# Add and GELU on one core: larger DMA rows, all loads ahead of all stores, and the adds on GpSimd

## The chip, the core and the metric

The kernel runs on one core of a Trainium2 chip. A core has several engines that run side by side, each with its own instruction stream: VectorE (DVE in the profile), ScalarE (ACT), GpSimd (POOL), TensorE (PE, not used here), and SyncE (SP), which here issues all DMA transfers. The transfers run on 16 DMA engines. Data lives in SBUF (128 partitions) and in PSUM, a smaller memory that VectorE and ScalarE can use too.

The metric is the device time of one execution, in microseconds (us). The kernel before has a median of 126.06 us over 11 runs (124.79 to 126.96).

## The reference

x and y are float32 arrays of 1024 rows by 4096 columns. The output has the same shape.

```python
z = x + y
out = 0.5 * z * (1 + tanh(sqrt(2 / pi) * (z + 0.044715 * z ** 3)))
```

This is the tanh form of GELU. Since 0.5 (1 + tanh(u)) = sigmoid(2u), it is z * sigmoid(c1 * z + root**2 * z**3), with c1 = 2 sqrt(2 / pi) and root**2 = c1 * 0.044715. The kernel computes it in this form.

## The kernel before, in words

Each partition holds 8 rows of an input one after the other, so 8 x 4096 = 32768 columns of float32 per partition, in one contiguous stretch of HBM (128 KB). The kernel cuts these columns into transfers and, within them, into chunks.

**Transfers.** The list `sizes` has 13 stretches of columns: 1024, 1024, 2048, six of 4096, 2048, 1024, 512, 512. Each stretch is loaded once from x (`load_x`, L73) and once from y (`load_y`, L80), and stored once (`store`, L83). A stretch of 4096 columns is 2 MB in rows of 16 KB, one row per partition. Each x stretch has its own resident tile, which the computation overwrites and which is then stored. y goes into four buffers of 4096 columns used in turn (`YB = 4`).

**Chunks.** The computation works on chunks of up to 1024 columns, 33 of them. For chunk c:

- `add` (L92): z = x + y, written over x. On GpSimd, except for the first two and the last two chunks, which are on VectorE (`by_pool`).
- `sq` (L97): ScalarE writes (root * z)**2 into a PSUM buffer w, of which there are four.
- `stt` (L100): VectorE makes w = (w + c1) * z.
- `sig` (L105): ScalarE makes w = sigmoid(w).
- `mul` (L108): VectorE writes z = w * z, over x.

**Order.** The order within each queue is written out by hand. ScalarE and VectorE follow a skewed order:

```python
for i in range(-3, C + 1):
    if 0 <= i < C:
        dve.append((stt, i))
        acts.append((sig, i))
    if 0 <= i - 1 < C:
        dve.append((mul, i - 1))
    if 0 <= i + 3 < C and i + 3 not in by_pool:
        dve.append((add, i + 3))
    if 0 <= i + 2 < C:
        acts.append((sq, i + 2))
```

So in ScalarE's queue the square of chunk i+1 stands ahead of the sigmoid of chunk i, and in VectorE's queue stt of i+1 stands ahead of mul of i. GpSimd has its adds in order of chunks.

SyncE's single queue holds loads and stores mixed: x and y of a stretch, then each store whose stretch ends at least `LEAD` = 8192 columns before the end of what has been loaded. A store that waits for its last mul holds up the loads behind it on this queue. The dictionary `needs` lists what each step must have behind it when the order is emitted; the semaphores between the engines are placed automatically, by the overlap of the regions that instructions read and write.

Of the kernel before, what the change touches and what calls it, by code (L numbers as in the profile page):

```python
# [1 line left out]

# [1 line left out]

# [4 lines left out]


@with_exitstack
def kernel(
    ctx: ExitStack,
    tc: tile.TileContext,
    x: bass.AP,
    y: bass.AP,
    out: bass.AP,
):

    nc = tc.nc
    P = nc.NUM_PARTITIONS
    fp32 = mybir.dt.float32
    act = mybir.ActivationFunctionType
    alu = mybir.AluOpType  # L30

    N, D = x.shape
    assert N % P == 0
    NB = N // P
    TOT = NB * D

    c1 = 2.0 * math.sqrt(2.0 / math.pi)
    root = math.sqrt(c1 * 0.044715)

    LEAD = 8192  # L40
    CH = 1024
    YB = 4
    sizes = [1024, 1024, 2048] + [D] * (NB - 2) + [2048, 1024, 512, 512]
    assert sum(sizes) == TOT
    starts = [sum(sizes[:t]) for t in range(len(sizes))]
    T = len(sizes)

    def hbm(ap, t):
        v = ap.rearrange("(p n) d -> p (n d)", p=P)
        return v[:, starts[t] : starts[t] + sizes[t]]  # L50

    chunks = []
    for t in range(T):
        o = 0
        while o < sizes[t]:
            f = min(CH, sizes[t] - o)
            chunks.append((t, o, f))
            o += f
    C = len(chunks)
    last = {t: c for c, (t, _, _) in enumerate(chunks)}  # L60
    by_pool = set(range(2, C - 2))

    xpool = ctx.enter_context(tc.tile_pool(name="xz", bufs=1))
    ypool = ctx.enter_context(tc.tile_pool(name="y", bufs=YB))
    ppool = ctx.enter_context(
        tc.tile_pool(name="w", bufs=4, space=bass.MemoryType.PSUM)
    )

    xt, yb, yt, wt = {}, {}, {}, {}

    def load_x(t):
        xt[t] = xpool.tile([P, sizes[t]], fp32, tag=f"x{t}", name=f"x{t}")
        nc.sync.dma_start(out=xt[t], in_=hbm(x, t))  # L73

    def load_y(t):
        n, o = divmod(starts[t], D)
        if o == 0:
            yb[n] = ypool.tile([P, D], fp32, tag="y", name=f"y{n}")
        yt[t] = yb[n][:, o : o + sizes[t]]
        nc.sync.dma_start(out=yt[t], in_=hbm(y, t))  # L80

    def store(t):
        nc.sync.dma_start(out=hbm(out, t), in_=xt[t])  # L83

    def z(c):
        t, o, f = chunks[c]
        return xt[t][:, o : o + f]

    def add(c):
        t, o, f = chunks[c]  # L90
        eng = nc.gpsimd if c in by_pool else nc.vector
        eng.tensor_add(out=z(c), in0=z(c), in1=yt[t][:, o : o + f])  # L92

    def sq(c):
        f = chunks[c][2]
        wt[c] = ppool.tile([P, CH], fp32, tag="w", name=f"w{c}")[:, :f]
        nc.scalar.activation(out=wt[c], in_=z(c), func=act.Square, scale=root)  # L97

    def stt(c):
        nc.vector.scalar_tensor_tensor(  # L100
            out=wt[c], in0=wt[c], scalar=c1, in1=z(c), op0=alu.add, op1=alu.mult
        )

    def sig(c):
        nc.scalar.activation(out=wt[c], in_=wt[c], func=act.Sigmoid)  # L105

    def mul(c):
        nc.vector.tensor_mul(out=z(c), in0=wt[c], in1=z(c))  # L108


    sp, pool, dve, acts = [], [], [], []
    s = 0
    for t in range(T):
        sp += [(load_x, t), (load_y, t)]
        while s < T and starts[s] + sizes[s] + LEAD <= starts[t] + sizes[t]:
            sp.append((store, s))
            s += 1
    sp += [(store, t) for t in range(s, T)]
    for c in range(C):
        if c in by_pool:  # L120
            pool.append((add, c))
    for i in range(-3, C + 1):
        if 0 <= i < C:
            dve.append((stt, i))
# [6 lines that stand above are left out]
            acts.append((sq, i + 2))  # L131

    needs = {
        load_x: lambda t: [],
        load_y: lambda t: [
            (add, c)
            for c, (i, _, _) in enumerate(chunks)
            if starts[t] % D == 0 and starts[i] // D == starts[t] // D - YB
        ],
        add: lambda c: [(load_y, chunks[c][0]), (load_x, chunks[c][0])],  # L140
        sq: lambda c: [(add, c)] + ([(mul, c - 4)] if c >= 4 else []),
        stt: lambda c: [(sq, c)],
        sig: lambda c: [(stt, c)],
        mul: lambda c: [(sig, c)],
        store: lambda t: [(mul, last[t])],
    }
    queues = [sp, pool, acts, dve]
    done = set()
    with tc.manual_schedule():
        one = xpool.tile([P, 1], fp32, tag="one", name="one")  # L150
        nc.vector.memset(one, 0.0)  # L151
        nc.scalar.activation(out=one, in_=one, func=act.Sigmoid)  # L152
        while any(queues):
            moved = False
            for q in queues:
                while q and all(n in done for n in needs[q[0][0]](q[0][1])):
                    fn, arg = q.pop(0)
                    fn(arg)
                    done.add((fn, arg))
                    moved = True  # L160
                    if q is not sp:
                        break
            assert moved, [q[:1] for q in queues]


# [1 line left out]
_INS = ['x', 'y']  # L167
_OUTS = [((1024, 4096), 'float32')]


# [23 lines left out]
```

## Time and profile before

| | |
|---|---|
| median of 11 runs | 126.06 us |
| the profiled execution's own time | 126.55 us |
| span of its profile (first to last instruction) | 124.8 us |
| data moved | 50.35 MB: 33.55 read, 16.78 written |
| mean DMA rate over the span | 404 GB/s |
| one GpSimd add of 1024 columns | 2348 ns |
| one stt, one mul of 1024 columns (VectorE) | 1231, 1213 ns |
| one square, one sigmoid of 1024 columns (ScalarE) | 1028, 983 ns |

The profile is taken from one execution. An engine's busy share is the part of the span in which it executes instructions. The page also cuts the span into 40 equal slices: each digit in a row is an engine's busy share in tenths, and the GB/s row is what the DMA engines moved. A group's row gives the source line, engine and operation, what it writes and reads, the shape, how often it ran, the total busy time and the mean time of one; then the engine's idle time just ahead of it and what ended most of that idle time. The chain that ended last is followed back from the last instruction through whatever released each step. The rows in order of time give the start, the duration, the engine, the line and the operation.

### The profile page before, as it was taken

To read this page: it belongs to the slowest core of one execution; us is meant where nothing else is said; L and a number is where in the kernel's file an instruction comes from. 1 tells how busy PE (TensorE), PEld (TensorE's weight loads), DVE (VectorE), ACT (ScalarE), POOL (GpSimd) and SP (SyncE) were. 2 spreads that over 40 slices of the span, in tenths; PEclk is the share of its full clock that TensorE was granted. 3 is DMA by queue.
4 is the path that set the end of the run, shared out by engine and by line. 5 is a ranking of instruction groups with operands and counts; after the bars stand their busy time and mean duration, and the time that the engine had idled before them with its cause. 6 is when DMAs were issued, how large, how long until landed. Compare 5 with 4: busy or idle time off the path is not lost.

```text
span 124.8 us, 301 instructions
## 1 busy us (share of the span) xinstructions
DVE 79.1 (63%) x71; ACT 64.2 (51%) x68; POOL 67.4 (54%) x33
## 2 busy tenths in 40 slices
DVE  0159259049989960299703996059940699899960
ACT  4036084068867820578206881078800887784610
POOL 0000680599899503996049940699307998960000
DMA  3999999999899999999999999999999999999494
GB/s 81 418 436 441 436 426 431 426 426 426 364 450 431 426 420 394 431 436 436 415 431 436 431 420 431 436 426 431 426 402 405 431 411 411 436 426 441 208 396 164
DMA packets 5618, 50.35 MB, mean 404 GB/s; under 512 B 624, under 2 KB 624, under 8 KB 2544
## 3 DMA queue, kind: packets, MB, share of 16 engines
q1 hardware_dynamic: 5616, 50.33, 96.7%
q14 instruction: 2, 0.02, 0.0%
HBM read 33.55 MB, written 16.78 MB: 403 GB/s over the span
## 4 chain that ended last, share of the span: by engine, by line
DMA 64%; POOL 15%; DVE 11%; SPq 3%; ACT 2%; issue 2%; POOLq 0%
DMA y<-in_y_dram 64%; POOL x L92 15%; DVE x L108 5%; DVE w L100 5%; SPq L73 2%; ACT w L97 2%; DVE x L92 1%; SPq L80 1%; ACT w L105 0%; SPq L83 0%; POOLq L92 0%
## 5 line engine op out<-in xcount | busy, mean ns | idle before, releaser
L92 POOL TENSOR_TENSOR x<-x,y 128x1024 f32<-128x1024 f32 x29 | 67.2, 2348 | 43.6 <-DMA y<-in_y_dram 43.6
L100 DVE SCALAR_TENSOR_TENSOR w<-w,x 128x1024 f32<-128x1024 f32 (+1 forms) x33 | 39.5, 1198 | 34.2 <-ACT w L97 34.2
L97 ACT ACTIVATE w<-x 128x1024 f32<-128x1024 f32 (+1 forms) x33 | 33.1, 1002 | 51.4 <-POOL x L92 44.9
L108 DVE TENSOR_TENSOR x<-w,x 128x1024 f32<-128x1024 f32 (+1 forms) x33 | 39.0, 1181 | 0.1
L105 ACT ACTIVATE w<-w 128x1024 f32<-128x1024 f32 (+1 forms) x33 | 31.6, 958 | 3.5 <-DVE w L100 3.4
L92 DVE TENSOR_TENSOR x<-x,y 128x1024 f32<-128x1024 f32 (+1 forms) x4 | 4.9, 1230 | 6.4 <-DMA y<-in_y_dram 6.4
L152 ACT ACT_TABLE_LOAD x1 | 1.3, 1283 | 0.7 <-PEq L178 0.7
L151 DVE MEMSET one<- 128x1 f32 x1 | 0.1, 59 | 0.8 <-PEq L178 0.8
L178 POOL MEMSET const-float32-0.0<- 128x1 f32 x1 | 0.1, 98 | 0.2 <-issue 0.2
L152 ACT ACTIVATE one<-one 128x1 f32<-128x1 f32 x1 | 0.2, 202 | 0.0
L178 POOL MEMSET const-bfloat16-1.0<- 128x1 bf16 x1 | 0.1, 102 | 0.0
L178 POOL MEMSET const-uint8-127<- 128x1 uint8 x1 | 0.1, 102 | 0.0
L178 POOL MEMSET const-float32-1.0<- 128x1 f32 x1 | 0.1, 98 | 0.0
## 6 DMA issues: line engine op xcount, KB each, us to landing
x<-in_x_dram SPq DMA_DIRECT2D x6, 2048.0 KB, 18.5
y<-in_y_dram SPq DMA_DIRECT2D x6, 2048.0 KB, 23.4
out_dram<-x SPq DMA_DIRECT2D x6, 2048.0 KB, 14.0
x<-in_x_dram SPq DMA_DIRECT2D x2, 1024.0 KB, 12.3
y<-in_y_dram SPq DMA_DIRECT2D x2, 1024.0 KB, 14.3
out_dram<-x SPq DMA_DIRECT2D x2, 1024.0 KB, 6.9
x<-in_x_dram SPq DMA_DIRECT2D x3, 512.0 KB, 5.4
y<-in_y_dram SPq DMA_DIRECT2D x3, 512.0 KB, 6.2
```

The costliest lines, as they stand in the source:

```text
L73: nc.sync.dma_start(out=xt[t], in_=hbm(x, t))
L80: nc.sync.dma_start(out=yt[t], in_=hbm(y, t))
L92: eng.tensor_add(out=z(c), in0=z(c), in1=yt[t][:, o : o + f])
L97: nc.scalar.activation(out=wt[c], in_=z(c), func=act.Square, scale=root)
L100: nc.vector.scalar_tensor_tensor(out=wt[c], in0=wt[c], scalar=c1, in1=z(c), op0=alu.add, op1=alu.mult)
L105: nc.scalar.activation(out=wt[c], in_=wt[c], func=act.Sigmoid)
L108: nc.vector.tensor_mul(out=z(c), in0=wt[c], in1=z(c))
L151: nc.vector.memset(one, 0.0)
L152: nc.scalar.activation(out=one, in_=one, func=act.Sigmoid)
L178: nc = _bacc.Bacc("TRN2", target_bir_lowering=False, num_devices=1)
```

## The change

The loads, the stores and the tiles are cut anew, and the order on SyncE's queue is changed; the arithmetic of a chunk stays.

- x has four loads, of 2048, 6144, 8192 and 16384 columns. y has five, of 2048, 6144, 8192, 8192 and 8192. There are four stores, of 16384, 8192, 4096 and 4096 columns. The largest rows are 64 KB, in the last load of x and in the first store.
- z is one resident tile of all 32768 columns, into which x is loaded. y has two buffers of 8192 columns in place of four of 4096. Both take the same SBUF in all.
- SyncE's queue holds all loads first (x0, y0, x1, y1, x2, y2, x3, y3, y4) and then all stores. y3 and y4 reuse the buffers of the first and second 8192 columns and wait for those adds.
- There are 32 chunks, each of 1024 columns. All adds but that of chunk 0 are on GpSimd.
- The skewed order on ScalarE and VectorE, and the four PSUM buffers, stay.

The core of the diff:

```diff
-    LEAD = 8192
+    YS = 8192
     CH = 1024
-    YB = 4
-    sizes = [1024, 1024, 2048] + [D] * (NB - 2) + [2048, 1024, 512, 512]
...
+    PS = 4
+    loads_x = [2048, 6144, 8192, 16384]
+    loads_y = [2048, 6144, 8192, 8192, 8192]
+    stores = [16384, 8192, 4096, 4096]
...
-    by_pool = set(range(2, C - 2))
...
+    cr = ranges([CH] * (TOT // CH))
+    C = len(cr)
+    by_pool = set(range(1, C))
...
+    pool_sb = ctx.enter_context(tc.tile_pool(name="xz", bufs=1))
+    pool_y = ctx.enter_context(tc.tile_pool(name="y", bufs=2))
...
+    zt = pool_sb.tile([P, TOT], fp32, tag="z", name="z")
...
+    def load_x(i):
+        a, b = xr[i]
+        nc.sync.dma_start(out=zt[:, a:b], in_=xv[:, a:b])
...
+    def load_y(i):
+        a, b = lr[i]
+        s, o = divmod(a, YS)
         if o == 0:
-            yb[n] = ypool.tile([P, D], fp32, tag="y", name=f"y{n}")
...
+            yt[s] = pool_y.tile([P, YS], fp32, tag="y", name=f"y{s}")
+        nc.sync.dma_start(out=yt[s][:, o : o + b - a], in_=yv[:, a:b])
...
+    def store(i):
+        a, b = sr[i]
+        nc.sync.dma_start(out=ov[:, a:b], in_=zt[:, a:b])
...
-    sp, pool, dve, acts = [], [], [], []
-    s = 0
-    for t in range(T):
-        sp += [(load_x, t), (load_y, t)]
-        while s < T and starts[s] + sizes[s] + LEAD <= starts[t] + sizes[t]:
-            sp.append((store, s))
-            s += 1
-    sp += [(store, t) for t in range(s, T)]
...
+    sp = []
+    for i, (a, b) in enumerate(lr):
+        sp += [(load_x, k) for k, r in enumerate(xr) if r[0] == a] + [(load_y, i)]
+    sp += [(store, i) for i in range(len(stores))]
...
     needs = {
...
-        store: lambda t: [(mul, last[t])],
+        store: lambda i: [(mul, c) for c in over(cr, *sr[i])],
     }
```

More of the change, by code (lines that the diff above doesn't have):

```diff
@@ L33 @@
     assert N % P == 0
-    NB = N // P
-    TOT = NB * D
+    TOT = N // P * D
+    xv, yv, ov = (a.rearrange("(p n) d -> p (n d)", p=P) for a in (x, y, out))
     c1 = 2.0 * math.sqrt(2.0 / math.pi)
     root = math.sqrt(c1 * 0.044715)
-    LEAD = 8192
+    YS = 8192
     CH = 1024
-    YB = 4
-    sizes = [1024, 1024, 2048] + [D] * (NB - 2) + [2048, 1024, 512, 512]
[L44 to L50, printed above, removed]
@@ L52 @@
-    chunks = []
-    for t in range(T):
[L54 to L60, printed above, removed]
-    by_pool = set(range(2, C - 2))
[L63 to L66, printed above, removed]
-    )
@@ L69 @@
[L69 to L76, printed above, removed]
-        if o == 0:
-            yb[n] = ypool.tile([P, D], fp32, tag="y", name=f"y{n}")
[L79 to L83, printed above, removed]
@@ L85, in z, with ranges @@
-    def z(c):
-        t, o, f = chunks[c]
-        return xt[t][:, o : o + f]
+    PS = 4
+    loads_x = [2048, 6144, 8192, 16384]
+    loads_y = [2048, 6144, 8192, 8192, 8192]
+    stores = [16384, 8192, 4096, 4096]
+    def ranges(sizes):
+        ends = [sum(sizes[: i + 1]) for i in range(len(sizes))]
+        assert ends[-1] == TOT
+        return [(e - f, e) for e, f in zip(ends, sizes)]
+    xr, lr, sr = ranges(loads_x), ranges(loads_y), ranges(stores)
+    cr = ranges([CH] * (TOT // CH))
@@ new lines, with over @@
+    C = len(cr)
+    by_pool = set(range(1, C))
+    def over(rs, lo, hi):
+        return [i for i, (a, b) in enumerate(rs) if a < hi and b > lo]
+    pool_sb = ctx.enter_context(tc.tile_pool(name="xz", bufs=1))
+    pool_y = ctx.enter_context(tc.tile_pool(name="y", bufs=2))
+    pool_w = ctx.enter_context(
+        tc.tile_pool(name="w", bufs=PS, space=bass.MemoryType.PSUM)
+    )
+    zt = pool_sb.tile([P, TOT], fp32, tag="z", name="z")
+    yt, wt = {}, {}
+    def load_x(i):
+        a, b = xr[i]
+        nc.sync.dma_start(out=zt[:, a:b], in_=xv[:, a:b])
@@ L89, in add @@
+    def load_y(i):
+        a, b = lr[i]
+        s, o = divmod(a, YS)
+        if o == 0:
+            yt[s] = pool_y.tile([P, YS], fp32, tag="y", name=f"y{s}")
[3 more added lines that the diff above has]
+        nc.sync.dma_start(out=ov[:, a:b], in_=zt[:, a:b])
     def add(c):
-        t, o, f = chunks[c]
+        a, b = cr[c]
+        s, o = divmod(a, YS)
         eng = nc.gpsimd if c in by_pool else nc.vector
-        eng.tensor_add(out=z(c), in0=z(c), in1=yt[t][:, o : o + f])
+        eng.tensor_add(out=zt[:, a:b], in0=zt[:, a:b], in1=yt[s][:, o : o + b - a])
@@ L94, in sq @@
     def sq(c):
-        f = chunks[c][2]
-        wt[c] = ppool.tile([P, CH], fp32, tag="w", name=f"w{c}")[:, :f]
-        nc.scalar.activation(out=wt[c], in_=z(c), func=act.Square, scale=root)
+        a, b = cr[c]
+        wt[c] = pool_w.tile([P, CH], fp32, tag="w", name=f"w{c}")
+        nc.scalar.activation(
+            out=wt[c], in_=zt[:, a:b], func=act.Square, scale=root
+        )
     def stt(c):
+        a, b = cr[c]
         nc.vector.scalar_tensor_tensor(
-            out=wt[c], in0=wt[c], scalar=c1, in1=z(c), op0=alu.add, op1=alu.mult
+            out=wt[c], in0=wt[c], scalar=c1, in1=zt[:, a:b], op0=alu.add, op1=alu.mult
@@ L107, in mul @@
     def mul(c):
-        nc.vector.tensor_mul(out=z(c), in0=wt[c], in1=z(c))
-    sp, pool, dve, acts = [], [], [], []
-    s = 0
-    for t in range(T):
-        sp += [(load_x, t), (load_y, t)]
-        while s < T and starts[s] + sizes[s] + LEAD <= starts[t] + sizes[t]:
-            sp.append((store, s))
-            s += 1
-    sp += [(store, t) for t in range(s, T)]
-    for c in range(C):
-        if c in by_pool:
-            pool.append((add, c))
+        a, b = cr[c]
+        nc.vector.tensor_mul(out=zt[:, a:b], in0=wt[c], in1=zt[:, a:b])
+    sp = []
+    for i, (a, b) in enumerate(lr):
+        sp += [(load_x, k) for k, r in enumerate(xr) if r[0] == a] + [(load_y, i)]
+    sp += [(store, i) for i in range(len(stores))]
+    pool = [(add, c) for c in range(C) if c in by_pool]
+    dve, acts = [], []
     for i in range(-3, C + 1):
@@ L133 @@
     needs = {
-        load_x: lambda t: [],
-        load_y: lambda t: [
+        load_x: lambda i: [],
+        load_y: lambda i: [
             (add, c)
-            for c, (i, _, _) in enumerate(chunks)
-            if starts[t] % D == 0 and starts[i] // D == starts[t] // D - YB
-        ],
-        add: lambda c: [(load_y, chunks[c][0]), (load_x, chunks[c][0])],
-        sq: lambda c: [(add, c)] + ([(mul, c - 4)] if c >= 4 else []),
+            for c in over(cr, lr[i][0] - 2 * YS, lr[i][0] - YS)
+            if lr[i][0] % YS == 0
+        ],
+        add: lambda c: [(load_x, i) for i in over(xr, *cr[c])]
+        + [(load_y, i) for i in over(lr, *cr[c])],
+        sq: lambda c: [(add, c)] + ([(mul, c - PS)] if c >= PS else []),
         stt: lambda c: [(sq, c)],
@@ L149 @@
     with tc.manual_schedule():
-        one = xpool.tile([P, 1], fp32, tag="one", name="one")
+        one = pool_sb.tile([P, 1], fp32, tag="one", name="one")
         nc.vector.memset(one, 0.0)
```

## The prediction

> **What bounds the kernel now.** I read the page's busy shares first, then the 40 slices and the DMA queue, the chain that ended last, the groups, and last the order of time round one load.
>
> ```profile
> DVE 79.1 (63%) x71; ACT 64.2 (51%) x68; POOL 67.4 (54%) x33
> ...
> DMA  3999999999899999999999999999999999999494
> GB/s 81 418 436 441 436 426 431 426 426 426 364 450 431 426 420 394 431 436 436 415 431 436 431 420 431 436 426 431 426 402 405 431 411 411 436 426 441 208 396 164
> ...
> q1 hardware_dynamic: 5616, 50.33, 96.7%
> ...
> DMA 64%; POOL 15%; DVE 11%; SPq 3%; ACT 2%; issue 2%; POOLq 0%
> ...
> L92 POOL TENSOR_TENSOR x<-x,y 128x1024 f32<-128x1024 f32 x29 | 67.2, 2348 | 43.6 <-DMA y<-in_y_dram 43.6
> L100 DVE SCALAR_TENSOR_TENSOR w<-w,x 128x1024 f32<-128x1024 f32 (+1 forms) x33 | 39.5, 1198 | 34.2 <-ACT w L97 34.2
> ```
>
> No compute engine is above 63%, while the DMA engines are busy in every slice from the second on, except a dip in the third slice from the end (208 GB/s). The chain is 64% DMA, and GpSimd's only large idle time (43.6 us) ends with a load of y. So the kernel is bound by its one DMA queue: 50.33 MB, of which nothing changes. What can change is how close the queue comes to its best rate, and what lies behind it at the end.
>
> How fast is the queue at best? The trace's packet records give the median time of one packet (one row on one of the 16 engines): 2 KB 85 ns, 4 KB 159 ns, 8 KB 309 ns, 16 KB 611 ns. From 8 to 16 KB, 8192 more bytes cost 302 ns, so a packet costs about 7 ns plus 36.9 ps a byte. Each engine carries 8 of a transfer's 128 rows.
>
> Where is it not at its best? The landing events give, for each transfer, the first and the last of its 16 engines. Before any store, the last engine lands at 3.3 us plus the packet time queued so far: the fourth transfer (4 x 8 x 159 ns = 5.1 us) at 8.36 us, the eighth (19.8 us by the same sum) at 23.13, the tenth (29.6 us) at 32.92. The engines are then 0.4 to 0.6 us apart. After that, at nearly each passage from a load of y to a store some packets are slow: at 30.1-31.9, 45.8-47.6, 60.9-61.6, 75.8-77.2 and 90.0-92.9 us, 57 packets of 16 KB and 15 us in all over the 16 engines. They don't fall evenly: the spread from first to last engine at the y load that closes each turn goes 0.4, 1.4, 1.9, 2.3, 3.1 us. The slowest engine sets the landing. The last y lands on its last engine at 109.22 us, where 3.3 us plus packets (103.5 us) would give 106.8: 2.4 us lost. The last store lands at 123.87, and the span ends 0.93 later. The dip to 208 GB/s is the faster engines having run out; the slowest one goes on (its stores land 114.14, 118.98, 121.41, 122.64, which are their own packet times apart). So before = 3.3 + 118.4 (packets) + about 2.4 (passages) + 0.9, within 0.3 of 124.8.
>
> The compute cadence, in order of time round one load:
>
> ```profile
> 23.26 9.27 POOL L92 TENSOR_TENSOR x<-x,y 128x1024 f32<-128x1024 f32 x4 [5.16 <-DMA y<-in_y_dram]
> 25.63 1.03 ACT L97 ACTIVATE w<-x 128x1024 f32<-128x1024 f32 x1 [5.55 <-POOL x L92]
> 26.60 0.98 ACT L105 ACTIVATE w<-w 128x1024 f32<-128x1024 f32 x1
> 26.69 1.23 DVE L100 SCALAR_TENSOR_TENSOR w<-w,x 128x1024 f32<-128x1024 f32 x1 [5.14 <-ACT w L97]
> 27.84 1.21 DVE L108 TENSOR_TENSOR x<-w,x 128x1024 f32<-128x1024 f32 x1
> ```
>
> Four adds take 9.27 us, 2.32 us a chunk; VectorE's pair stt and mul starts 1.15 us apart, 2.30 a chunk. ScalarE has the square of chunk c queued ahead of the sigmoid of c-1, so the mul of a load's last chunk comes only after the next load's first add (here the mul at 27.84 belongs to the chunk before). That matters below.
>
> **What the Trainium skill says.** "DMA: Bandwidth & Descriptors", section "Where 436 GB/s comes from", derives 435 GB/s from 16 ports; the slices peak at 436-441, and 16 KB in 611 ns on 16 engines is 429. Its section "Queues, rings and completion order" says that every engine consumes its own ring in order; the growing spread agrees. "SBUF — State Buffer", section "Who interferes with whom", says a VectorE instruction with at most one SBUF input doesn't contend with GpSimd, one with two does. stt and mul have w in PSUM: the adds beside them took 2337 to 2367 ns, all 29. The VectorE add of 512 columns that ran beside GpSimd took 1794 ns, the other 676. "GPSIMD Engine Reference", section "Performance versus the Vector engine", has the add 1.96 times slower on GpSimd; here 2348 against 1225 ns.
>
> **The change part by part.**
>
> *Rows.* By the fit a row of 24 KB takes 0.913 us, 32 KB 1.215, 64 KB 2.423. An engine's 8 rows: loads 2 x 2.47 (8 KB), 2 x 7.30 (24 KB), 2 x 9.72 (x2, y2), 19.38 (x3), 2 x 9.72 (y3, y4), together 77.8 us; stores 19.38 + 9.72 + 4.89 + 4.89 = 38.9. Sum 116.7 against 118.4: 1.7 us less. Rows above 16 KB are not in the trace; for 64 KB I bound the packet between 2.41 us (no fixed cost) and 10% more than the fit, and take the fit.
>
> *Order.* One passage from loads to stores in place of about six: of the 2.4 us lost on the slowest engine, at most one passage's worst growth of the spread, 1.0 us, should stay.
>
> *Waits on the queue.* y3 needs a y buffer: the adds of chunks 0-7. y1 lands at 3.3 + 19.5 = 22.8; six adds later it is 36.9, while the queue holds work until x3's end (61.7 less 0.9). y4 needs the adds of 8-15: y2 lands 42.3, plus 8 x 2.32 is 61.0; y3 keeps the engines to 70.5. Both hidden, by 24 and 9 us. A wait of these also holds all stores behind it on SP, but none could go yet. Without that cover each late microsecond would be an idle one.
>
> *Landings.* x3 61.7, y3 71.4, y4 81.1, and with a queue never empty store 0 100.5, store 1 110.2, store 2 115.1, store 3 120.0.
>
> *Stores against compute.* A DMA issued to an idle queue lands its last engine about 2.55 us plus its packets after issue (the first x: issued 0.74, 1.27 us of packets, landed 4.57; the last store, issued at about 120.6 with 0.69 us of packets, landed 123.87, agrees). Store 0 needs mul 15, which stands behind square 16 and stt 16, so behind y3: add 16 71.5 to 73.9, square to 74.9, stt to 76.2, mul 15 done 77.3; with the 2.55 it could run from 79.9, the queue reaches it at 81.1. Hidden by 1.2 us. Store 1 needs mul 23: add 24 ends 92.4, mul 23 95.9, ready 98.5 against 100.5. Store 2: mul 27 at 105.2, ready 107.7 against 110.2. Store 3: GpSimd runs 16 adds without a gap, 71.5 + 16 x 2.32 = 108.7; square 109.7, stt 111.0, sigmoid 112.0, mul 31 done 113.2; ready 115.8 against 115.1. Late by 0.7 us: the end is set by GpSimd's run, not by the queue: 115.8 + 4.89 = 120.7, plus 0.93 is a **span of 121.6**. A passage loss of up to 0.7 us is hidden under it, since it delays only the queue; of 1.0 us it would show 0.3.
>
> *The rest.* Two 512-column chunks and four VectorE adds become 32 equal chunks with one VectorE add, at the start, before GpSimd has work: the contended add above is gone. The first add waits for 8.2 us in place of 5.9; hidden, since y1 is what comes next. The last store is 2 MB in place of 0.25 MB: counted (4.89 us after the last mul). In PSUM four buffers stay four.
>
> Against the profiled 124.8: minus 3.2 us. Its execution took 126.55, so 1.75 lies outside the span: 123.3. The median of the runs is 0.49 below that execution; as part of that may be luck in the passages, I take about half: **123.1 us**, 2.3% faster.
>
> **The rivals.**
>
> *The queue sets the end after all.* The passage costs 1 to 3 us, or store 0's 1.2 us of cover is eaten because the fast engines run dry before y4's slowest ends. Last landing 121.0 to 123.0, time 123.7 to 125.7. For it: after the first, a passage widened the spread by 0.4 to 1.0 us. Against it: one passage.
>
> *GpSimd is slower in a long run.* Its 16 adds set the end; at 2.42 us each the span is 123.2, time 124.9; at 2.52 it equals before. For it: no run of 16 is in the trace, the longest unbroken ones are four. Against: 29 adds within 30 ns.
>
> *The slower side: 64 KB rows are slow.* x3 and store 0 are 38.8 us of packets. Load and store each a share f slower put the queue's end at 120.9 + 38.8 f: equal to before at f = 10% (390 GB/s), and at f = 15% a span of 126.7, time 128.5. For it: nothing above 16 KB was measured. Against: the time per byte falls steadily from 2 to 16 KB.
>
> *The change doesn't do what it says.* If the waits are kept for z as a whole, add 0 waits for x3 at 61.7 and 32 adds follow: 136, then 4.5 and 4.9 and 2.6 + 0.9, about 150. Against: y's first buffer is filled by three loads, and the first add starts at 5.92, before the third landed at 13.33; and adds and muls of one x tile overlap.
>
> **How the numbers follow.** Forecast as worked (span 120.9 to 122.2, time 122.0 to 123.7): 66 in 100. Queue sets the end: 14, all faster but its last tenths. Slow GpSimd run: 8, of which half is faster and half within 0.5% or slower. Slow 64 KB rows: 9, of which 6 slower. Tracking as a whole: 3. A measurement can't tell less than about 0.5% (0.6 us) from no change: faster is below 125.4, slower above 126.7. Faster 0.84, same 0.06, slower 0.10. The range 122.0 to 125.2 takes in the forecast and most of the first two rivals.
>
> **What would show it.** Right: one unbroken row of full DMA slices to the end; 64 KB packets near 2.42 us; y3 landing near 71.4; 16 adds in a row in 37.2 us; the chain ending GpSimd, ScalarE, VectorE, store 3; store 3 landing near 120.7. Wrong: a DMA dip near 80 us (store 0 late), a spread over 1.5 us at y4, packets of 64 KB over 2.6 us, or a GpSimd add over 2.4 us.

## The result, and the profile after

| | before | after |
|---|---|---|
| median | 126.05 us (124.58 to 126.96, 47 runs) | 122.96 us (122.83 to 123.47, 12 runs) |
| profiled execution, and its span | 126.55, 124.8 us | 122.95, 121.2 us |
| ratio | | 0.9813, 95% interval 0.9781 to 0.9844 |

By the ratio the change makes the kernel 1.9% faster, by the medians 3.1 us or 2.5%: the ratio leaves out the slow runs of the kernel before, 16 of 47, which lie more than 1.5% above its fastest. The executions of the kernel before scatter over 2.4 us, those of the kernel after over 0.6, and the profiled execution of the kernel before took 0.5 us more than its median, so the two spans differ by more than the medians. The forecast was 123.1 us, with a span of 121.6.

The page of the kernel after: busy shares, the DMA slices and rates, the queue, the chain that ended last, and two groups.

```profile
DVE 75.5 (62%) x66; ACT 63.8 (53%) x66; POOL 73.0 (60%) x35
...
DMA  4999999898989977978798989897997798989992
GB/s 89 422 441 495 414 389 495 371 519 346 519 346 519 519 346 346 692 346 346 346 519 346 519 346 519 346 519 346 633 411 346 346 498 368 508 357 427 427 433 97
...
q1 hardware_dynamic: 1872, 50.33, 97.1%
...
DMA 45%; DVE 32%; POOL 13%; SPq 1%; ACT 1%; issue 0%; POOLq 0%
...
L89 POOL TENSOR_TENSOR z<-z,y 128x1024 f32<-128x1024 f32 x31 | 72.8, 2387 | 35.0 <-DMA y<-in_y_dram 35.0
L100 DVE SCALAR_TENSOR_TENSOR w<-w,z 128x1024 f32<-128x1024 f32 x32 | 39.4, 1232 | 29.3 <-ACT w L94 29.3
```

The same 50.33 MB move in 1872 packets in place of 5616. There is no dip near the end any more. The rates that jump between 346 and 519 GB/s are no stalls: a row of 64 KB takes 2.42 us, a slice is 3.03 us, and a packet is counted whole in one slice. Rows of 32 and 64 KB are better read by landings.

The rows in order of time from the landing of y3 on, again of the kernel after:

```profile
71.25 36.99 POOL L89 TENSOR_TENSOR z<-z,y 128x1024 f32<-128x1024 f32 x16 [10.55 <-DMA y<-in_y_dram]
...
75.83 1.21 DVE L109 TENSOR_TENSOR z<-w,z 128x1024 f32<-128x1024 f32 x1
...
77.07 36.16 SPq L83 DMA_DIRECT2D out_dram<-z  x4
...
110.47 2.39 DVE L109 TENSOR_TENSOR z<-w,z 128x1024 f32<-128x1024 f32 x2
```

GpSimd does its 16 adds without a gap. The mul that ends at 77.04 is that of chunk 15, and store 0 is issued right after it. The last mul ends at 112.86, and store 3 is issued then.

The landing events, last of the 16 engines, beside the forecast:

| | forecast us | measured us |
|---|---|---|
| y3, y4 | 71.4, 81.1 | 71.12, 80.98 |
| mul 15, mul 31 done | 77.3, 113.2 | 77.04, 112.86 |
| store 0, 1, 2 | 100.5, 110.2, 115.1 | 100.81, 110.46, 115.31 |
| store 3 | 120.7, set by mul 31 | 120.14, right behind store 2 |

Packets have medians of 0.912 (24 KB), 1.213 (32 KB) and 2.418 us (64 KB), where the line through 8 and 16 KB gave 0.913, 1.215 and 2.423. The spread between the first and the last engine stays at 0.3 to 0.5 us through all loads, and goes to 1.0 at the one passage from loads to stores.

### The profile page after: what moved, and what is told of

Read it like the earlier page. It is cut to its first block, busy times and chain, and to the rows that moved or that the text cites. A ratio compares the mean times of both kernels' runs of the same rounds, so it can differ in the third digit from the quotient of the medians.

```text
span 121.2 us, 241 instructions
## 1 busy us (share of the span) xinstructions
DVE 75.5 (62%) x66; ACT 63.8 (53%) x66; POOL 73.0 (60%) x35
## 3 DMA queue, kind: packets, MB, share of 16 engines
q1 hardware_dynamic: 1872, 50.33, 97.1%
## 4 chain that ended last, share of the span: by engine, by line
DMA 45%; DVE 32%; POOL 13%; SPq 1%; ACT 1%; issue 0%; POOLq 0%
DMA y<-in_y_dram 45%; DVE z L109 16%; DVE w L100 16%; POOL z L89 13%; ACT w L94 1%; SPq L72 1%; SPq L79 0%; POOLq L89 0%
## 5 line engine op out<-in xcount | busy, mean ns | idle before, releaser
L89 POOL TENSOR_TENSOR z<-z,y 128x1024 f32<-128x1024 f32 x31 | 72.8, 2387 | 35.0 <-DMA y<-in_y_dram 35.0
L100 DVE SCALAR_TENSOR_TENSOR w<-w,z 128x1024 f32<-128x1024 f32 x32 | 39.4, 1232 | 29.3 <-ACT w L94 29.3
L94 ACT ACTIVATE w<-z 128x1024 f32<-128x1024 f32 x32 | 32.9, 1028 | 46.7 <-POOL z L89 39.6
L109 DVE TENSOR_TENSOR z<-w,z 128x1024 f32<-128x1024 f32 x32 | 38.8, 1214 | 0.0
L105 ACT ACTIVATE w<-w 128x1024 f32<-128x1024 f32 x32 | 31.4, 981 | 0.4 <-DVE w L100 0.4
L89 DVE TENSOR_TENSOR z<-z,y 128x1024 f32<-128x1024 f32 x1 | 1.2, 1226 | 7.3 <-DMA y<-in_y_dram 7.3
## 6 DMA issues: line engine op xcount, KB each, us to landing
z<-in_x_dram SPq DMA_DIRECT2D x1, 3072.0 KB, 13.7
```

What stands on the lines that cost most here:

```text
L89: eng.tensor_add(out=zt[:, a:b], in0=zt[:, a:b], in1=yt[s][:, o : o + b - a])
L94: nc.scalar.activation(out=wt[c], in_=zt[:, a:b], func=act.Square, scale=root)
L100: nc.vector.scalar_tensor_tensor(out=wt[c], in0=wt[c], scalar=c1, in1=zt[:, a:b], op0=alu.add, op1=alu.mult)
L109: nc.vector.tensor_mul(out=zt[:, a:b], in0=wt[c], in1=zt[:, a:b])
```

## The experiments

### Which part of the change brings the gain: the rows or the order

`rows16` keeps the order of the kernel after and goes back to rows of 16 KB:

```diff
-    loads_x = [2048, 6144, 8192, 16384]
-    loads_y = [2048, 6144, 8192, 8192, 8192]
-    stores = [16384, 8192, 4096, 4096]
+    loads_x = [2048, 2048] + [4096] * 7
+    loads_y = [2048, 2048] + [4096] * 7
+    stores = [4096] * 8
```

with y in four buffers of 4096 columns.

> The kernel after with the old row size: x and y in loads of 2048, 2048 and seven of 4096 columns, eight stores of 4096, y in four buffers of 4096; all loads still ahead of all stores. My theory: packets 117.4 us against 116.7, one passage: last landing 3.3 + 117.4 + 0.5 = 121.2, span 122.1, time 123.8; the order alone brings three quarters of the gain, and the runs scatter as little as those of after (0.6 us). Rival (the gain is in the rows): 125 or more, and the scatter of before (over 2 us).

Measured: 123.68 us (123.57 to 124.05), ratio to before 0.9786 (0.974 to 0.9832), span 121.8. The DMA slices and rates of its page:

```profile
DMA  4999999999999999999999999999999999999992
GB/s 91 420 425 430 441 430 430 430 430 430 430 430 430 430 430 430 430 430 425 430 430 430 425 430 428 422 409 436 430 430 436 436 430 430 430 436 430 430 430 113
```

With 16 KB rows the picture is plain: a flat 430 GB/s, and one shallow place, 422 and 409, at the passage, between 76 and 82 us. The runs scatter over 0.5 us, as expected. By the medians `rows16` has 2.3 of the 3.05 us (126.01 to 123.68), and the rows from 16 KB to the new sizes bring the other 0.7, as the packets' sum had it (117.4 against 116.7).

But the 2.3 us are not the order alone. The kernel before also has rows of 2 and 4 KB, and its packets come to 118.4 us, so about 1.0 of the 2.3 us is again packets. About 1.3 us are left for the order, the equal chunks and GpSimd's adds together. No run takes over the order and keeps the old chunks, so these three are not separated. The trace of the kernel before speaks for the order: up to the end its slowest engine lands one store after another, from 114.14 to 123.87 us, each its own packet time behind the last, so the shape of the last chunks did not set its end there. And the loss differs between executions: the fastest of the kernel before in that comparison, 124.81 us, less 1.0 of packets is 123.8, and `rows16` took 123.57 to 124.05. By this estimate the fastest executions lose next to nothing by the old order; no trace of one was kept.

`rows32` cuts only the 64 KB transfers in two:

```diff
-    loads_x = [2048, 6144, 8192, 16384]
-    stores = [16384, 8192, 4096, 4096]
+    loads_x = [2048, 6144, 8192, 8192, 8192]
+    stores = [8192, 8192, 8192, 4096, 4096]
```

> The kernel after, with its 64 KB transfers cut in two: x in loads of 2048, 6144 and three of 8192 columns, stores of 8192, 8192, 8192, 4096 and 4096. My theory (a packet is about 7 ns and 36.9 ps a byte, the order counts): 32 packets of 64 KB per engine become 64 of 32 KB, 0.1 us more in all, and there is still one passage from loads to stores: 123.0 us, the same as after, 122.96. Rival (the 64 KB rows are what wins): at least 1 us slower than after, 124 or more.

Measured: 123.37 us (123.26 to 123.74), ratio 0.9762 (0.9716 to 0.9808). That is 0.4 over after, where the packets explain 0.1, and far from the rival's 1 us; two of the twelve runs of after, 123.45 and 123.47, lie in the same range. The landings of its profile, taken from the slowest of the four runs, show the place: y4 lands 10.54 us after the x load ahead of it, for packets of 9.7. Shortly after 78 us 16 packets of y4, as many as there are engines, took 0.64 us too long on average. In the kernel after eight did, by 0.25 us. What differs there is that the first store, of 8192 columns, needs only mul 7 and stands in the queue from 61 us, in place of 77. The next runs ask whether that is the reason.

### The kernel after once more, and store 0 issued earlier

> The kernel after, unchanged, as the measure for the three that follow: 122.9 to 123.1.

Measured: 123.02 us (122.82 to 123.15), ratio 0.9811 (0.9756 to 0.9865).

`sig_first` takes store 0 out of its wait for y3:

```diff
             acts.append((sq, i + 2))
+    a, b = acts.index((sig, 15)), acts.index((sq, 16))
+    acts[a], acts[b] = acts[b], acts[a]
+    a, b = dve.index((mul, 15)), dve.index((stt, 16))
+    dve[a], dve[b] = dve[b], dve[a]
```

> The kernel after with sigmoid 15 ahead of square 16 on ScalarE and mul 15 ahead of stt 16 on VectorE, so that store 0 no longer waits for y3: it can be issued near 66 us in place of 77. My prediction (store 0 was covered by the queue): no change, within 0.2 us. Rival 1 (store 0 came late, the faster engines ran dry): 0.3 to 0.5 faster. Rival 2 (the slow packets near 78.8 us come from the issue of store 0 at 77.1 and not from the passage): they move to about 67 us.

Measured: 123.56 us (123.36 to 123.78), ratio 0.9855 (0.9786 to 0.9923): 0.5 slower than the kernel after in the same comparison, whose runs end at 123.15. Of the sixteen runs of the kernel after in both comparisons, two (123.45 and 123.47) reach into this range. None of the three expectations came true. The order of time on SyncE's queue confirms the edit, which issues the stores from 65.42 on:

```profile
60.79 0.33 SPq L79 DMA_DIRECT2D y<-in_y_dram  x1
65.42 47.87 SPq L83 DMA_DIRECT2D out_dram<-z  x4
```

The slow packets did not move to 67 us, so the issue itself does not make them: they are still among the last two packets that each engine has of y4, starting at 77.45 to 79.92 us. But they became more. Counted from 0.05 us over the median of their size, they are 31 with 16.8 us of excess in all. Where store 0 is issued at 77.0 to 77.2 us and the queue is otherwise the same, four profiles have 8 with 2.0 us (after), 4 with 0.6 (after again), 25 with 6.2 and 17 with 7.1 (`late_600` and `late_2300`, described below). `rows32`, early as well, has 26 with 11.1. y4 lands at 81.93 us here and at 81.85 in `rows32`, against 80.98 to 81.44 in those four. So in these traces a store that already stands behind the last load goes with a slower end of that load; a store that comes just in time does so less, but by how much differs widely between executions.

`y4_16k` and `y4_16k_early` are the kernel after and `sig_first` with y4 in two loads:

```diff
-    loads_y = [2048, 6144, 8192, 8192, 8192]
+    loads_y = [2048, 6144, 8192, 8192, 4096, 4096]
```

> The kernel after with its last load of y in two of 4096 columns, rows of 16 KB. If the loss at the passage is that of the last one or two load packets of each engine and goes with their length, 0.2 us less than after (123.0): 122.8. If not, 123.0 to 123.1 for the eight more packets.

> sig_first (store 0 issued near 65 us, 123.56) with the same two loads of 16 KB rows. If the loss goes with the length of the last packets: 123.2 or less. If an early issue costs the same whatever the rows: 123.6.

Measured: 123.07 us (122.86 to 123.21, ratio 0.9752, interval 0.9686 to 0.9819) and 123.28 us (123.1 to 123.51, ratio 0.977, 0.969 to 0.985). With the store issued early, shorter last rows are 0.3 us below `sig_first`, with runs that overlap (123.36 to 123.78 there) and stem from another comparison. The traces point the same way: about as many packets are slow (28), but each by 0.36 us in place of 0.54. With the store issued late the hoped-for 0.2 us did not come. So a gain from shorter last rows is likely where the store is early, and not shown. Why few packets are slow in one kernel or execution and most in another is not settled: `rows16` also has its stores issued early (from 52.3 us), and only ten of its packets are slow, by 2.6 us in all.

### What sets the end

`late_600` and `late_2300` put one more GpSimd add, on a scratch tile, ahead of the add of chunk 28:

```diff
+    def extra(c):
+        nc.gpsimd.tensor_add(out=ex, in0=ex, in1=ex)
...
     pool = [(add, c) for c in range(C) if c in by_pool]
+    pool.insert(pool.index((add, 28)), (extra, 0))
...
+        ex = pool_sb.tile([P, 256], fp32, tag="ex", name="ex")
```

`late_2300` has 1024 in place of 256.

> The kernel after with one more GpSimd add of 256 columns, on a scratch tile, ahead of the add of chunk 28 (it changes nothing in the result): mul 31 comes about 0.6 us later. As predicted (the run of adds sets the end): all of it shows, 123.5. Rival (the queue sets the end, by a margin m): 0.6 less m; with m of 0.6 or more no change.

> The same with 1024 columns, some 2.3 us. As predicted: 125.2. Rival: 125.2 less the margin m, so that the two runs together give m.

Measured: 123.02 us (122.97 to 123.2, ratio 0.9815, interval 0.9762 to 0.9868) and 123.86 us (123.84 to 123.94, ratio 0.988, 0.9827 to 0.9933), against 123.02 for the kernel after. The first delay costs nothing, and of the second 0.84 us shows. How long the delays really were stands in GpSimd's order of time, here of `late_2300`:

```profile
71.28 27.74 POOL L89 TENSOR_TENSOR z<-z,y 128x1024 f32<-128x1024 f32 x12 [10.55 <-DMA y<-in_y_dram]
99.00 1.88 POOL L92 TENSOR_TENSOR ex<-ex 128x1024 f32<-128x1024 f32 x1
100.85 9.26 POOL L89 TENSOR_TENSOR z<-z,y 128x1024 f32<-128x1024 f32 x4
```

The extra add took 1.88 us and not 2.3; in `late_600` it took 0.60. Counted from the start of the run of adds, the last mul is done after 41.61 and 41.65 us in the two profiles of the kernel after, 42.17 in `late_600` and 43.45 in `late_2300`. So the delays were 0.5 and 1.8 us, and the queue sets the end of the kernel after, with a margin of about 1.0 us (1.8 less 0.84). The time from issue to landing gives the same by another way. The order of time of `late_2300`:

```profile
106.66 8.44 SPq L83 DMA_DIRECT2D out_dram<-z  x2
...
112.34 2.39 DVE L112 TENSOR_TENSOR z<-w,z 128x1024 f32<-128x1024 f32 x2
```

The second of the two stores ends its issue at 115.10; an issue takes 0.33 us, so it began at 114.77, right after the last mul (114.73). It landed at 121.04. Take off 4.89 us of packets, and 1.38 us lie between issue and landing. Here the queue was empty and the whole of it shows. Two other profiles below have a store that found the queue empty, `two_passages` (issued 115.32, landed 121.58, 4.89 of packets) with 1.37 us and `halves_apart2` (issued 117.85, landed 121.73, 2.47 of packets) with 1.41. In the kernel after, store 3 was issued at 112.89 us, so by this it was ready at 114.27, 1.0 before store 2 landed at 115.31.

### Is it the passages from loads to stores

`two_passages` is `rows32` with its first store ahead of its last load of x:

```diff
     sp += [(store, i) for i in range(len(stores))]
+    sp.remove((store, 0))
+    sp.insert(sp.index((load_x, 4)), (store, 0))
```

> rows32 (123.37) with its first store moved in between y3 and x4: two passages from loads to stores, both while the engines are still close together. Theory of the spread: the second passage costs what a first one does, 0.4 to 1.0 us, 123.8 to 124.4. Rival (passages are free, all loads first gains in another way): 123.4.

Measured: 124.24 us (124.2 to 124.51), ratio 0.9851 (0.9784 to 0.9918), 0.87 over `rows32`: the number that I expected, but at most in part for the reason. The slow packets do stand where the theory puts them: 32 at 58.1 to 60.5 us, 13.7 us of excess in all, at the end of y3, which now has a store behind it. In `rows32` y3 ends at the same place with a load behind it, and there no packet near it is over by more than 0.08 us. But the second passage, at the end of y4, has only two slow packets, and the two passages together lose on the queue what the one of `rows32` lost: the last but one store lands at 116.19 us in the one profile, at 116.24 in the other. Between these two profiles the time is lost behind that. Store 4 lands at 121.58, 5.39 us later for 4.89 of packets, with all engines within 0.2 us: the queue had run empty. GpSimd's order of time shows why:

```profile
62.57 18.52 POOL L89 TENSOR_TENSOR z<-z,y 128x1024 f32<-128x1024 f32 x8 [1.86 <-DMA y<-in_y_dram]
92.15 18.51 POOL L89 TENSOR_TENSOR z<-z,y 128x1024 f32<-128x1024 f32 x8 [11.06 <-DMA y<-in_y_dram]
```

y4 has 4 MB of stores ahead of it and lands at 92.02, eight adds follow, and the last mul is done at 115.29. `rows32` has y4 at 81.85. But between these two profiles only 0.5 of the 0.87 us lies: the profiled execution of `rows32`, 123.74 us, is 0.4 above its median, that of `two_passages`, 124.25, is at its own. Against a median execution of `rows32` the second passage can still have cost up to 0.4 us on the queue.

The other three runs go back to the kernel before. `halves_adjacent` is the control: each store of 4096 columns among the loads becomes two halves (`store_half`), one behind the other. `halves_apart` puts the load of y between the halves:

```diff
         sp += [(load_x, t), (load_y, t)]
         while s < T and starts[s] + sizes[s] + LEAD <= starts[t] + sizes[t]:
-            sp.append((store, s))
+            if sizes[s] == D and sp[-1] == (load_y, t):
+                sp.insert(len(sp) - 1, (store_half, (s, 0)))
+                sp.append((store_half, (s, 1)))
+            else:
+                sp.append((store, s))
             s += 1
```

`halves_apart2` is the same, but keeps the halves together at the very last load.

> The kernel before with each store of 4096 columns that stands among the loads issued as two halves of 2048, one right behind the other, so that the number of passages between loads and stores stays: the control for the next one. All theories: 0.3 us for the smaller rows, 126.0 to 126.7.

> The same two halves, but the load of y stands between them, so that the passages from loads to stores double from about six to eleven. My theory (each passage costs the slowest engine 0.4 to 1.0 us): 2 to 3 us over the control, about 128.5. Rival (a passage costs nothing, the losses come from elsewhere): the same as the control within 0.5 us.

> halves_apart again, but with the two halves of the last such store kept together, so that the last load of y is no longer held back by half a store; ten passages in place of five among the large transfers, the end as in the control. Theory as first put (each passage costs 0.4 to 1.0 us): still 2 us over the control, 128. Theory as the last runs have it (the loss stops growing once the 16 engines are spread over 2 to 3 us; the 1.0 us of halves_apart came from its late last load): the control's 126.2, within 0.3.

Measured: 126.19 us (125.27 to 127.41, ratio 1.0029, interval 0.9995 to 1.0063), 127.19 us (125.94 to 128.04, ratio 1.0084, 1.0052 to 1.0116) and 127.3 us (126.16 to 127.91, ratio 1.0111, 1.008 to 1.0143). Twice the passages cost about 1 us over the control (1.0 and 1.1 by the medians, 0.7 and 1.0 by the ratios), half or less of what I had expected. And in the profiles of the control and of `halves_apart2` even this is not lost on the queue. The last load of y lands on its last engine at 108.96 us in the control and at 108.40 in `halves_apart2`; the last 2 MB store at 118.73 and 118.14. Up to there the kernel with twice the passages is 0.6 us ahead; the profiled execution of the control, 126.58 us, is 0.4 above its median, the other, 127.24, is at its own, so at the medians the two queues are about equal. The spread is 2.7 us in the control and 1.8 there. `halves_apart2` falls behind afterwards, waiting for mul. GpSimd's order of time, the control first, then `halves_apart2`:

```profile
94.03 9.26 POOL L98 TENSOR_TENSOR x<-x,y 128x1024 f32<-128x1024 f32 x4 [5.43 <-DMA y<-in_y_dram]
103.86 6.96 POOL L98 TENSOR_TENSOR x<-x,y 128x1024 f32<-128x1024 f32 x3 [0.57 <-DMA y<-in_y_dram]
```

```profile
95.97 16.18 POOL L98 TENSOR_TENSOR x<-x,y 128x1024 f32<-128x1024 f32 x7 [5.38 <-DMA y<-in_y_dram]
```

The last 2 MB load of y now has half a store ahead of it and lands 1.9 us later (95.84 against 93.90). From there GpSimd has no gap left to catch up in, VectorE ends at 121.5 in place of 120.2, and the queue runs empty. My expectation for `halves_apart2` blamed the wrong load: I had freed the last one, and it was the last large one.

So the place is shown and the price is not. Slow packets stand, with few exceptions, at the end of a load that has a store behind it; one exception is six packets of an 8 KB store near 37 us in the kernel before. But a price of 0.4 to 1.0 us for every passage is not borne out: ten in place of five made the queue no later, and the second of two cost it 0.4 us at most, with one trace each. What the kernel before does lose on the queue, 2.4 us on its slowest engine in its profile, builds up with the spread over its turns of loads and stores, to 3.1 us; with all loads first the spread stays at 0.8 to 1.2 us. Why a later passage costs little is open; no run here holds the spread fixed.

What both edits cost in the traces came by another way: a store ahead of a load makes the load land later by the store's length, and the compute behind that load then reaches past the queue. In the kernel before the same chain runs close behind the queue: y8, its last 2 MB load of y, lands on its slowest engine at 94.28 us, and the last mul ends at 120.54. The store issued at 116.89 was ready at 118.27 by the 1.38 us above, an estimate, and the store ahead of it landed at 118.98: 0.7 us to spare. All loads first takes the stores out of the loads' way: in `rows16` the last y lands at 82.09 us in place of 109.22.

## Why the prediction was right

**The rows: right.** The line through the packets of 8 and 16 KB held up to 64 KB, within 5 ns. 1.7 us were forecast for all rows, and the part that a run separates, from 16 KB to the new sizes, was 0.7 as forecast. The other 1.0, for the rows of 2 and 4 KB, is inside the gain of `rows16` and was not measured by itself. One reading of the page was off without bearing on the sum: the slices do not peak at 441, one reads 450, right behind one of 364.

**The order: near in size, too simple as a rule.** The loss of 2.4 us on the slowest engine was forecast to shrink to 1.0 at most, so by 1.4 or more. At the one passage left, store 0 lands 19.83 us behind y4 for 19.35 of packets: 0.5. By the medians about 1.3 us are left for the order with the equal chunks, once the 1.0 of packets is taken off the 2.3 of `rows16`. But the loss of the kernel before isn't about six equal prices, as the doubling shows. The forecast's term "one passage in place of about six" came near the sum by a rule that the runs don't bear out; as far as the rule goes, that is luck. The 2.4 us were also read from one execution, 0.5 us slower than the median.

**The waits for y's buffers: right.** y4 was forecast to be issued at 61.0 and was at 60.73, hidden as said.

**Store 0: right that it is hidden, for too small a margin.** I had 1.2 us. With 1.4 us from issue to landing in place of 2.55 it is 81.1 - 77.3 - 1.4 = 2.4. `sig_first` shows that coming earlier is no gain and even a loss, which nothing in my working foresaw.

**The end: wrong.** "Late by 0.7 us: the end is set by GpSimd's run, not by the queue" is the step that failed, and in it the 2.55 us between issue and landing (beside the packets). I took it from the first load, whose first packets are slow (up to 0.85 us too long at 1.8 us), and from the last store, which stood behind another one in the queue; both include waiting that isn't the issue's. A store issued to an empty queue took 1.4 us over its packets. Store 3 was therefore ready at 114.3 us and not at 115.8; 1.2 of this is the wrong 2.55, the rest the last mul, which was done 0.3 earlier. Late by 0.7 became early by 1.0, and the queue, which I had ending at 120.0, set the end at 120.14. So the span came out 0.4 us shorter than forecast. In the time more than half of that was made up by the 0.25 us that I took off for luck: two errors with opposite signs, and that 123.1 came so near to 122.96 is in part luck.

**GpSimd's cadence: right.** 16 adds took 36.99 us, forecast 37.2. That rival, the slow 64 KB rows, and the tracking of z as a whole fell with the first profile of the kernel after. The rival of the queue setting the end was right about the mechanism and wrong about its price: it had the last landing at 121.0 to 123.0, measured was 120.14.

## What to carry to other kernels

When a kernel is bound by one DMA queue, add up the packets per engine and compare with the landings of the first and the last engine: what the landings are late is what an order of transfers can win, and rows larger than 16 KB win only their few nanoseconds a packet, 0.7 us here. The chain that ended last does not see the queue: in the kernel after it ends in 38 us of VectorE, yet 0.5 us more in that chain cost nothing, because the store behind it had to wait for the store ahead. Take the time from issue to landing only from a transfer that found the queue empty, and don't issue the first store long before the loads ahead of it are done merely because it can be: `sig_first` was 0.5 us slower for it. Before two profiles are set side by side, compare each profiled execution with the median of its kernel; here two controls were 0.4 us above theirs, as much as some of the effects looked for. And measure a delay in the trace before it is used as a yardstick: the add meant to take 2.3 us took 1.88.

## What the runs showed of the hardware that I had not expected

- Where a store stood in the queue early (issued 65.4 us), the last two packets of the load ahead were slow on nearly every engine: 31 packets, 16.8 us in all, with rows of 32 KB. Where it was issued at 77.0 to 77.2 us, four profiles have 4 to 25 such packets and 0.6 to 7.1 us. The kernel with the early store was 0.5 us of 123 slower.
- Loads with a store behind them end slowly, but the loss is no fixed price for each: two passages ended the queue where one did (116.19 and 116.24 us), and ten were no later than five (118.14 and 118.73), in one profile each and within the 0.4 us by which the controls' profiles lie above their medians.
- A store that found the queue empty landed 1.37 to 1.41 us after its issue, beside its packets, in three profiles.
- The merged first store gains by its date, not by its 64 KB rows, as far as these runs tell: `rows32` and `sig_first`, without and with such rows and both early, are within 0.2 us of each other.
